# Waiting for the last four stores in a second section of SyncE alone

## The chip, the cores and the metric

One core of a Trainium2 chip. The metric is device time in microseconds (us) of one execution. "Span" is the time from the first to the last of the program's own instructions in a profiled execution; the device time is longer than it, by 1.79 us on average in the 11 runs of the kernel before that were timed beside e1. The same kernel scatters by more than the change is expected to be worth (the same 11 runs lie between 210.50 and 211.92 us), so the argument rests on the instruction records of the profiles, and the timed runs are a check.

## The reference

```python
# x [16, 512, 1024], weight [1024, 768], bias [768], residual [16, 512, 768], all float32
def reference(x, weight, bias, residual):
    return (np.matmul(x, weight) + bias + residual).astype(np.float32)
```

## The kernel before

The rows of x (8192 of 1024) go through the core in 64 tiles of 128. Each is cast to bf16, transposed on TensorE, multiplied by the weights, and finished by VectorE (with additions on GpSimd). SyncE issues all transfers. The kernel first collects its operations in a list and then emits them in one section of all engines, with waits that it works out itself; every transfer gets a semaphore (a counter that engines can wait for) of its own, which its landing raises by 16 (that of the last store rises 16 times in the trace, from 206.243 to 207.725). A section ends with a row of small instructions, called its exit here. In the trace of this kernel SyncE raises a signal at 208.036 us, every engine answers it with a DRAIN and a semaphore at about 208.1 (drains start at 208.074 to 208.126), SyncE collects the answers with two waits (208.211 and 208.270) and passes a NOP (208.336, 13 ns).

The store part and the end (cuts marked with "..."):

```python
# the order of the stores: kind, block, first and last row group (and a cut in partitions)
 ... ('s', 0, 0, 16), ... ('s', 1, 0, 16), ... ('s', 2, 0, 16), ('s', 3, 0, 10), ('s', 3, 10, 11, 104),
 ('s', 3, 11, 13), ('s', 3, 13, 14), ('s', 3, 14, 15), ('c', 3, 15, 0), ('c', 3, 15, 1)]

    def emit(self):                         # of the class Program
        ...                                 # which waits are already known to be over
        for n, (eng, emit, _, dma) in enumerate(ops):
            e = self.engines[eng]
            for d in waits[n]:
                e.wait_ge(*mark[d])
            if emit is None:                # the collecting operation: waits only
                continue
            ins = emit(e)
            if dma:
                sem = self.tc.alloc_semaphore(f"landed_{n}")
                mark[n] = (sem, 16)
                ins.then_inc(sem, 16)
            ...

                    dma(out_d[S, p0:p1, j0:j1, n0:n0 + nl],            # a store
                        R[p0:p1, t0 % RR:t0 % RR + j1 - j0, n0:n0 + nl],
                        rows(t0, t0 + j1 - j0, cs), [("out", len(stores))])
                    stores.append(("out", len(stores)))
    ...
    op("sp", None, stores)                  # SyncE waits for all stores
    with tc.tile_critical():                # one section of all engines
        prog.emit()
# the tile context closes here: drain, barrier, clearing of semaphores, barrier
```

There are eleven stores (the one with a cut counts twice). The last four are a row group of 384 KB, another, and the two pieces of the last row group, 256 KB and 128 KB.

Of the kernel before, what the change touches and what calls it, by code (L numbers as in the profile page):

```python
# [14 lines left out]
RR = 32  # L15
# [18 lines left out]
 ('r', 2, 6, 16), ('s', 1, 0, 16), ('x', 3, 0, 6), ('r', 3, 0, 7), ('x', 3, 6, 16),  # L34
 ('r', 3, 7, 16), ('s', 2, 0, 16), ('s', 3, 0, 10), ('s', 3, 10, 11, 104), ('s', 3, 11, 13),
 ('s', 3, 13, 14), ('s', 3, 14, 15), ('c', 3, 15, 0), ('c', 3, 15, 1)]
LAST = [(0, 512), (512, 256)]


class Program:  # L40
# [10 lines left out]
    def add(self, eng, emit, rd=(), wr=(), dma=False):  # L51
        n, ops = len(self.ops), self.ops
        deps = {self.writer[k] for k in (*rd, *wr) if k in self.writer and (eng != "pe" or ops[self.writer[k]][0] != eng)}
        for k in wr:
            deps.update(d for d in self.readers.get(k, ()) if ops[d][0] != eng or ops[d][3])
        for k in rd:
            self.readers.setdefault(k, set()).add(n)
        for k in wr:
            self.writer[k], self.readers[k] = n, set()
        self.ops.append((eng, emit, deps - {n}, dma))  # L60

    def emit(self):
        ops, known = self.ops, {e: {} for e in self.engines}
        lane, count, snap, waits = [], {}, [], []
        for n, (eng, _, deps, dma) in enumerate(ops):
            mine = (n, 0) if dma else (eng, count.setdefault(eng, 0) + 1)
            if not dma:
                count[eng] += 1
            seen = known[eng]
            need = {}  # L70
            for d in deps:
                f, i = lane[d]
                if seen.get(f, -1) < i and i > need.get(f, (-1, 0))[0]:
                    need[f] = (i, d)
            need = {
                f: (i, d) for f, (i, d) in need.items()
                if not any(snap[d2].get(f, -1) >= i for g, (_, d2) in need.items() if g != f)
            }
            for f, (i, d) in need.items():
                for g, v in (*snap[d].items(), (f, i)):  # L80
                    if seen.get(g, -1) < v:
                        seen[g] = v
            waits.append([d for _, d in need.values()])
            lane.append(mine)
            own = dict(seen)
            own[mine[0]] = mine[1]
            snap.append(own)
        told = {d for w in waits for d in w}
        sems = {e: self.tc.alloc_semaphore(f"done_{e}") for e in self.engines if e != "sp"}
        total, mark = dict.fromkeys(self.engines, 0), {}  # L90
        for n, (eng, emit, _, dma) in enumerate(ops):
            e = self.engines[eng]
            for d in waits[n]:
                e.wait_ge(*mark[d])
            if emit is None:
                continue
            ins = emit(e)
            if dma:
                sem = self.tc.alloc_semaphore(f"landed_{n}")
                mark[n] = (sem, 16)  # L100
                ins.then_inc(sem, 16)
            elif n in told:
                total[eng] += 1
                mark[n] = (sems[eng], total[eng])
                ins.then_inc(sems[eng], 1)


@with_exitstack
def kernel(
# [8 lines left out]
    nc = tc.nc  # L118
# [33 lines left out]
    prog = Program(tc)  # L152
    op = prog.add

    def rows(a, b, cs=range(len(chunks))):
        return [("R", r % RR, c) for r in range(a, b) for c in cs]

    def dma(dst, src, rd, wr):
        op("sp", lambda e: e.dma_start(out=dst, in_=src), rd, wr, dma=True)  # L159
# [3 lines left out]
    stores = []  # L163

    def pump():
        while queue:
            kind, S, j0, j1, *cut = queue[0]
            if kind == "c":
                need = [("outc", j1)]
            elif kind in ("w", "b"):  # L170
                need = []
            elif kind == "x":
                need = [("cast", t - XR) for t in range(J * S + j0, J * S + j1) if t >= XR]
            elif kind == "r":
                need = [("store", t - RR) for t in range(J * S + j0, J * S + j1) if t >= RR]
                at = [t % RR for t in range(J * S + j0, J * S + j1)]
                if S < RR // J and any(W_ROW <= r < W_ROW + 2 * n_q for r in at):
                    need.append(("wcast", n_q - 1))
                if S < RR // J:
                    need += [("add", t) for t in range(EARLY_END) if TMP_ROW + t in at]  # L180
            else:
                need = [("out", J * S + j) for j in range(j0, j1)]
            if not all(n in done for n in need):
                return
            queue.pop(0)
            t0, nj = J * S + j0, j1 - j0
            if kind == "b":
                dma(bias_row.rearrange("(g p) n -> g p n", p=QUAD)[:, 0, :],
                    bias[None, :].to_broadcast([P // QUAD, N]), [], ["bias_row"])
                continue  # L190
            if kind == "w":
                dma(w_st[:, 2 * S + j0:2 * S + j1, :], w_d[:, S, j0:j1, :], [],
                    rows(W_ROW + 2 * S + j0, W_ROW + 2 * S + j1))
                continue
            if kind == "x":
                dma(X[:, t0 % XR:t0 % XR + nj, :], x_d[S, :, j0:j1, :], [],
                    [("X", t % XR) for t in range(t0, t0 + nj)])
            elif kind == "r":
                dma(R[:, t0 % RR:t0 % RR + nj, :], res_d[S, :, j0:j1, :], [], rows(t0, t0 + nj))
            else:  # L200
                n0, nl = (0, N) if kind == "s" else LAST[j1]
                cs = range(len(chunks)) if kind == "s" else [j1]
                j1 = j1 if kind == "s" else j0 + 1
                edges = [0, *cut, P]
                for p0, p1 in zip(edges, edges[1:]):
                    dma(out_d[S, p0:p1, j0:j1, n0:n0 + nl],
                        R[p0:p1, t0 % RR:t0 % RR + j1 - j0, n0:n0 + nl], rows(t0, t0 + j1 - j0, cs), [("out", len(stores))])
                    stores.append(("out", len(stores)))
                done.update(("store", J * S + j) for j in range(j0, j1))
            done.update((kind, J * S + j) for j in range(j0, j1))  # L210

    def mark(*what):
        done.add(what)
        pump()
# [31 lines left out]
    def times(po, lhsT, rhs, first, final, rd, wr):  # L246
        def emit(e):
            return e.add_instruction(mybir.InstMatmult(  # L248
                name=nc.get_next_instruction_name(),
                ins=[e.lower_ap(rhs), e.lower_ap(lhsT, for_matmul_weights=True)], outs=[e.lower_ap(po)],  # L250
                start_tensor_calc=first, stop_tensor_calc=final,
                tile_size=(P, P), tile_position=(0, 0), ldweights=False,
            ))
        op("pe", emit, rd, wr)
# [46 lines left out]
    def dummies(n, i):  # L301
# [10 lines left out]
        out=ident, in_=ident, compare_op=mybir.AluOpType.not_equal, fill=1.0, base=0,  # L312
        pattern=[[-1, P]], channel_multiplier=1,
    ), ["ident"], ["ident"])
    dummies(WARM, 0)

    pump()
    for kind, *a in HEAD_ORDER:
        if kind == "bias":
# [15 lines left out]
        else:  # L335
            mm_all(a[0], [a[1]])
    pump()
    for t in range(HEAD - 1):
        if ("fin", t) not in done:
# [11 lines left out]
    t = n_t - 1  # L351
    for i, (n0, nl) in enumerate(LAST):
        b = (t - 2 * i) % HEAD
# [5 lines left out]
    mark("out", t)  # L359
    pump()  # L360
    assert not queue, queue
    op("sp", None, stores)
    with tc.tile_critical():  # L363
        prog.emit()


# [28 lines left out]
```

## Time and profile before

| | before |
|---|---|
| device time, first measurement, median of 4 runs | 210.88 us (210.72 to 211.20) |
| span of the profiled run | 209.394 us |
| last matmul ends | 204.088 us |
| the last store's landing (16th increment of its semaphore) | 207.725 us |
| from that landing to the end of the span | 1.669 us |

The prediction shows the lines of the profile that carry this, and how to read them. The times with three decimals are from the single instruction and semaphore records of the same trace.

### The profile page before, as it was taken

What the parts mean: (1) busy time and instruction counts of PE and PEld (TensorE: products, weight loads), DVE (VectorE), ACT (ScalarE), POOL (GpSimd) and SP (SyncE); (2) the same over time, 40 slices, a digit from 0 to 9 for tenths busy, and PEclk for the clock granted to TensorE, in tenths of its full rate; (3) what the DMA queues carried; (4) which work ended last, traced back from release to release, by engine and by line L of the source; (5) the groups of instructions that cost most, each with busy time, mean ns of one, the idle gap of its engine ahead of it and who ended that gap; (6) DMA issues with size and microseconds to landing.
All of it is one profiled execution on the core that took longest, in us unless ns stands there. A gap on an engine that the chain in (4) does not pass through costs nothing.

```text
span 209.4 us, 2487 instructions
## 1 busy us (share of the span) xinstructions
PE 202.3 (97%) x1298; PEld 81.2 (39%) x794; DVE 105.3 (50%) x141; ACT 66.2 (32%) x69; POOL 115.2 (55%) x71
## 2 busy tenths in 40 slices
PE   7999999999999999999999999999999999999990
PEld 2433433443444344344434433443444344334440
DVE  1458555445545554554455454645544554554460
ACT  2444513412740372310370083320190055330000
POOL 1100029759999805998039702999108940999000
PEclk9999999999999999999999999999999999999999
DMA  6999999999989899999999999999999999998993
GB/s 214 426 425 440 434 417 467 389 446 419 491 376 501 379 438 393 441 446 416 419 446 480 394 411 495 404 394 421 434 469 415 446 404 475 432 451 382 417 364 145
DMA packets 4924, 87.20 MB, mean 416 GB/s; under 512 B 557, under 2 KB 685, under 8 KB 1841
## 3 DMA queue, kind: packets, MB, share of 16 engines
q1 hardware_dynamic: 4913, 87.05, 97.6%
q8 instruction: 8, 0.13, 0.3%
q14 instruction: 3, 0.02, 0.0%
HBM read 61.88 MB, written 25.17 MB: 416 GB/s over the span
## 4 chain that ended last, share of the span: by engine, by line
PE 92%; DMA 4%; DVE 1%; SPq 0%; ACT 0%; issue 0%
PE psum_o L248 79%; PE pt L241 13%; DMA x_tile<-in_x_dram 4%; SPq L159 0%; DVE xt L217 0%; ACT xb L217 0%; DVE ro L220 0%; SPq L390 0%; SPq L363 0%
## 5 line engine op out<-in xcount | busy, mean ns | idle before, releaser
L248 PE MATMUL psum_o<-w_sb,xt 128*128 128x256 bf16 (+1 forms) x1024 | 176.6, 326 | 0.3 <-DVE xt L217 0.3
L220 POOL TENSOR_TENSOR ro<-ro,bias_sb 128x768 f32<-128x768 f32 x50 | 88.9, 1813 | 46.7 <-DMA ro<-in_residual_dram 46.7
L217 ACT CAST xb<-x_tile 128x1024 bf16<-128x1024 f32 (+1 forms) x63 | 61.4, 1023 | 117.1 <-DMA x_tile<-in_x_dram 81.8
L259 PEld LDWEIGHTS <-xt 128*128 128x128 bf16 x520 | 50.9, 98 | 102.5 <-issue 100.5
L217 DVE COPY xt<-pt 128x1024 bf16<-128x1024 bf16 x64 | 44.1, 691 | 84.0 <-PE pt L241 84.0
L220 DVE TENSOR_TENSOR ro<-psum_o,ro 128x768 f32<-128x768 f32 (+2 forms) x51 | 47.6, 934 | 6.3 <-POOL ro L220 4.3
L241 PE MATMUL pt<-ident,xb 128*128 128x128 f32 x256 | 38.7, 275 | 0.2 <-ACT xb L217 0.2
L220 POOL TENSOR_TENSOR ro<-ro 128x768 f32<-128x768 f32 x14 | 25.0, 1818 | 25.0 <-DMA ro<-in_residual_dram 25.0
L241 PEld LDWEIGHTS pt<-ident,xb 128*128 128x128 f32 x256 | 30.1, 142 | 15.4 <-issue 12.3
L220 DVE TENSOR_TENSOR ro<-psum_o,bias_sb 128x768 f32<-128x768 f32 x14 | 13.2, 948 | 0.0
L303 PE MATMUL psum_o<-warm 128*128 128x512 bf16 x18 | 6.9, 546 | 1.4 <-DVE warm_a L223 1.4
L217 DVE CAST xb<-x_tile 128x512 bf16<-128x512 f32 (+1 forms) x4 | 1.9, 492 | 5.8 <-DMA x_tile<-in_x_dram 5.8
L217 ACT CAST w_sb<-ro 128x768 bf16<-128x768 f32 x4 | 3.3, 832 | 3.7 <-DMA ro<-in_weight_dram 3.7
L217 POOL CAST w_sb<-ro 128x768 bf16<-128x768 f32 x1 | 0.8, 824 | 6.0 <-DMA ro<-in_weight_dram 6.0
L303 PEld LDWEIGHTS psum_o<-warm 128*128 128x128 bf16 x18 | 2.2, 127 | 4.7 <-issue 3.0
L217 DVE CAST w_sb<-ro 128x768 bf16<-128x768 f32 x3 | 1.7, 558 | 2.0 <-DMA ro<-in_weight_dram 2.0
L217 ACT ACT_TABLE_LOAD x1 | 1.3, 1283 | 0.9 <-SPq L363 0.9
L320 DVE STREAM_SHUFFLE bias_sb<-bias_row 128x768 f32<-128x768 f32 x1 | 1.0, 1008 | 0.0
L223 DVE MEMSET warm<- 128x256 uint32 x1 | 0.3, 272 | 1.1 <-SPq L363 1.1
L223 DVE MEMSET bias_row<- 128x768 f32 x1 | 0.7, 698 | 0.1
L223 POOL MEMSET ident<- 128x128 f32 x1 | 0.2, 205 | 0.5 <-SPq L363 0.5
L311 POOL TENSOR_SCALAR_AFFINE_SELECT ident<-ident 128x128 f32<-128x128 f32 x1 | 0.3, 294 | 0.2 <-POOL ident L223 0.2
(7 smaller groups left out, 0.7 us busy)
## 6 DMA issues: line engine op xcount, KB each, us to landing
out_dram<-ro SPq DMA_DIRECT2D x3, 6144.0 KB, 34.4
x_tile<-in_x_dram SPq DMA_DIRECT2D x3, 5120.0 KB, 24.5
ro<-in_residual_dram SPq DMA_DIRECT2D x3, 3840.0 KB, 32.0
x_tile<-in_x_dram SPq DMA_DIRECT2D x3, 3072.0 KB, 39.8
ro<-in_residual_dram SPq DMA_DIRECT2D x3, 2304.0 KB, 18.5
x_tile<-in_x_dram SPq DMA_DIRECT2D x4, 1024.0 KB, 10.9
x_tile<-in_x_dram SPq DMA_DIRECT2D x2, 2048.0 KB, 23.3
out_dram<-ro SPq DMA_DIRECT2D x1, 3840.0 KB, 13.1
```

The lines of the kernel that those rows point to most:

```text
L217: op(eng, lambda e: (e.copy if eng == "act" else e.tensor_copy)(out=dst, in_=src), rd, wr)
L220: op(eng, lambda e: e.tensor_add(out=dst, in0=a, in1=b), rd, wr)
L223: op(eng, lambda e: e.memset(dst, v), [], [wr])
L241: op("pe", lambda e, q=q: e.transpose(out=pt[:, q, :], in_=words[:, ts(q, P)], identity=ident), [("XB", t % XB_N, 2 * q // n_q), "ident"], ...
L248: return e.add_instruction(mybir.InstMatmult(name=nc.get_next_instruction_name(), ins=[e.lower_ap(rhs), e.lower_ap(lhsT, for_matmul_weight ...
L259: op("pe", lambda g: g.ldweights(lhsT), rd)
L303: op("pe", lambda e: e.matmul(PO[i][:, 0:512], lhsT=warm[:, 0:P], rhs=warm, start=True, stop=True), ["warm"], [("PO", i)])
L311: op("pool", lambda e: e.affine_select(out=ident, in_=ident, compare_op=mybir.AluOpType.not_equal, fill=1.0, base=0, pattern=[[-1, P]], ch ...
L320: op("dve", lambda e: e.stream_shuffle(out=bias_sb, in_=bias_row, mask=[0] * QUAD), ["bias_row"], ["bias"])
```

## The change

Its intent: SyncE waits at the end of the big section only for the first seven stores. The section then closes, with all its drains and answers, while the last four stores are still in flight, and these are awaited in a second section that names SyncE alone, the last store first.

```diff
+OUTSIDE = 4
-    def emit(self):
+    def emit(self, ends):
...
-            if emit is None:
-                continue
             ins = emit(e)
...
+        return [mark[n] for n in ends]
...
-                        R[...], rows(...), [("out", len(stores))])
-                    stores.append(("out", len(stores)))
+                        R[...], rows(...), [])
+                    stores.append(len(prog.ops) - 1)
...
-    op("sp", None, stores)
     with tc.tile_critical():
-        prog.emit()
+        landed = prog.emit(stores)
+        for sem, value in landed[:-OUTSIDE]:
+            nc.sync.wait_ge(sem, value)
+    with tc.tile_critical(sync_engine=mybir.EngineType.SP):
+        for sem, value in reversed(landed[-OUTSIDE:]):
+            nc.sync.wait_ge(sem, value)
```

More of the change, by code (lines that the diff above doesn't have):

```diff
@@ L206, in pump @@
                     dma(out_d[S, p0:p1, j0:j1, n0:n0 + nl],
-                        R[p0:p1, t0 % RR:t0 % RR + j1 - j0, n0:n0 + nl], rows(t0, t0 + j1 - j0, cs), [("out", len(stores))])
-                    stores.append(("out", len(stores)))
+                        R[p0:p1, t0 % RR:t0 % RR + j1 - j0, n0:n0 + nl], rows(t0, t0 + j1 - j0, cs), [])
+                    stores.append(len(prog.ops) - 1)
                 done.update(("store", J * S + j) for j in range(j0, j1))
```

## The prediction

> **What bounds the kernel now.** I read the page from the top, then the stretch after the last matmul in growing detail, because the change touches only what SyncE does there.
>
> First the page's head and its chain of work.
>
> ```profile
> span 209.4 us, 2487 instructions
> PE 202.3 (97%) x1298; PEld 81.2 (39%) x794; DVE 105.3 (50%) x141; ACT 66.2 (32%) x69; POOL 115.2 (55%) x71
> ...
> PE 92%; DMA 4%; DVE 1%; SPq 0%; ACT 0%; issue 0%
> ```
>
> TensorE is busy for 202.3 of 209.4 us and carries 92% of the chain; its clock row reads 9 in every slice. None of these instructions is touched. What can move is the part in which TensorE is idle, and only the end of it: 209.4 - 202.3 = 7.1 us are idle in all, some of them at the start (first matmul at 1.4 us) and 5.3 at the end. The table of busy time by stretch shows the end:
>
> ```profile
> 203.00:204.10 1.10, 1.09 (x9) 0.69 (x7) 0.69 (x1) 0.00 (x0) 0.00 (x0) 1.00 1.00 405
> 204.10:205.00 0.90, 0.00 (x0) 0.00 (x0) 0.42 (x1) 0.00 (x0) 0.00 (x0) 1.00 0.83 330
> 205.00:206.00 1.00, 0.00 (x0) 0.00 (x0) 0.00 (x0) 0.00 (x0) 0.00 (x0) 1.00 0.98 373
> 206.00:207.00 1.00, 0.00 (x0) 0.00 (x0) 0.00 (x0) 0.00 (x0) 0.00 (x0) 1.00 0.29 102
> 207.00:208.00 1.00, 0.00 (x0) 0.00 (x0) 0.00 (x0) 0.00 (x0) 0.00 (x0) 1.00 0.02 8
> 208.00:209.40 1.40, 0.00 (x0) 0.00 (x0) 0.00 (x0) 0.00 (x0) 0.00 (x0) 0.73 0.00 0
> ```
>
> The columns are the stretch, its length, busy time of PE, PEld, DVE, ACT and POOL, granted clock, DMA share and GB/s. Matmuls end at 204.1, the last addition of VectorE at 204.55 (0.42 us from 204.125), and after that only bytes and semaphores move: nearly no data after 207, none after 208, and still the program ends at 209.4. So the last 5.3 us fall into three parts: last addition and store (to about 207.7), and then roughly 1.7 us without data or compute. That last part is the subject.
>
> The instructions of the waiting line, of the section's line and of the line that closes the program, from 204 us on, say what it consists of:
>
> ```profile
> L94 SPq EVENT_SEMAPHORE  x4: 28/28/28, 205.8 to 207.8; - x4
> L363 SPq COMPARE_BRANCH  x1: 33/33/33, 207.9 to 207.9; - x1
> L363 ACTq DRAIN  x1: 8/8/8, 208.1 to 208.1; - x1
> L363 POOLq DRAIN  x1: 41/41/41, 208.1 to 208.1; - x1
> L363 SPq EVENT_SEMAPHORE  x3: 17/28/28, 208.0 to 208.3; - x3
> L363 SPq NOP  x1: 13/13/13, 208.3 to 208.3; - x1
> ...
> L390 SPq DRAIN  x3: 7/7/7, 208.4 to 208.7; - x3
> L390 POOLq EVENT_SEMAPHORE_RANGE_CLEAR  x1: 287/287/287, 208.8 to 208.8; - x1
> L390 POOLq EVENT_SEMAPHORE  x4: 17/17/17, 208.5 to 209.3; - x4
> ```
>
> Each row has durations (least, median, most) in ns and the first and last start in us. L94 are SyncE's waits for the stores; L363 is the section's exit, in which SyncE tells every engine to drain and collects the answers; L390 closes the whole program: a barrier, the clearing of the semaphores by GpSimd, a second barrier. The rows of waits of SyncE's queue say that the stores set the start of it:
>
> ```profile
> SPq L94 <- DMA out_dram<-ro: 2.7, 3, 0.9
> SPq L390 <- PEq L390: 0.8, 2, 0.6
> ```
>
> The single instruction records give the order to the nanosecond. The last store (128 KB) is issued at 204.578 and its 16th and last increment comes at 207.725, 3.15 us later, and 0.76 us after the 15th. Then: wait at 207.741, one more wait at 207.806, branch at 207.873, signal to all engines 208.036, SyncE's own drain 208.126, two collecting waits at 208.211 and 208.270, closing NOP 208.336, first drain of the program's end 208.411, its barrier 208.474, end 209.394. From the landing to the end: 0.311 us of waits and branch (207.725 to 208.036), 0.375 us of section exit (208.036 to 208.411), 0.983 us of program end. Sum 1.669 us.
>
> [...]the drains and waits report 7 to 28 ns on SyncE, but successive ones start 59 to 90 ns apart, so I count starts, not durations. [...]the last store's semaphore rises 16 times between 206.243 and 207.725, and SyncE goes on at 207.741. [...]
>
> **The change part by part.**
> 1. The stores no longer write a key of their own, and the collecting operation at the end is gone. No other operation read those keys, so no wait elsewhere changes. Worth 0.
> 2. At the end of the first section SyncE now waits for the first seven of eleven stores. Before, nine waits stood there (the first two of the eleven had been awaited by later loads): four instructions with two waits each, and one on the branch. Of the seven, the last to land is the store of two rows: its semaphore's last increment came at 204.860, and SyncE itself is busy until 204.967 with issuing the last store. So these waits find everything done. Three or four instructions of about 0.065 us, a branch of 0.163 us and the exit of 0.375 us: 204.97 + 0.26 + 0.16 + 0.38 = about 205.8. All of this runs while the last four stores are in flight.
> 3. Entry to the second section: a NOP and a branch, as at the program's beginning (NOP at 0.720, branch at 0.796, first DMA issue at 0.949: 0.23 us). 205.8 + 0.23 = 206.0. The last landing is at 207.725, so 1.7 us of slack: it hides, even if the entry cost three times that.
> 4. Four waits, in reverse order, so that the last store's semaphore is asked first, with the next to last. Two instructions or one and the branch: landing 207.725, wait 207.741, second 207.806, branch 207.873, next 208.036. That is the very sequence of before, where the last landing also was followed by exactly one more wait and the branch. Gain 0 (0.065 at most, if the packing leaves one instruction less).
> 5. The exit of a section of SyncE alone. This is where I expect the gain. The two collecting waits (208.211 and 208.270) have nobody to collect: 208.336 - 208.211 = 0.125 us. If the signal to the engines and SyncE's drain on its own signal go too, 208.211 - 208.036 = 0.175 us more. So 0.125 to 0.300, middle 0.21.
> 6. The program's end: 0.983 us, unchanged. The other engines' drains for its first barrier came at 208.157 to 208.193 and would now come near 205.9, but that barrier opens only with SyncE's at 208.474, so earlier arrivals are worth nothing. The clearing gets a few semaphores more: 46 of them took 0.239 us from first to last, 5.3 ns each; one to five more cost 0.01 to 0.03 us.
>
> Sum: -0.21 + 0.02 = -0.19 us, from 210.84 to 210.65 us, 0.09%.
>
> **The rivals.** The first is that the second section's exit goes to all engines after all. For it: the exit of the first section serves all engines, and the drains of the program's end are there in any case. Against it: the section names SyncE alone, and nothing of another engine stands in it. Time: then step 5 is worth 0, and with step 6's clearing it is 210.86.
>
> The second is that the whole exit and some of the program's end hide behind the stores, as the intent of the change suggests: 0.375 us of exit, or even the first barrier too. For the exit: SyncE may need only a NOP after its waits. Against the barrier: the page's chain and the waits show SyncE as the last to arrive in it, and SyncE must still wait for the stores before. Time: 210.84 - 0.37 = 210.47, and no view speaks for more.
>
> The third is a cost that I can't see beforehand: the second block begins elsewhere in SyncE's stream[...]. SyncE runs only 57 instructions within the span and its branches took 0.15 and 0.16 us here, so no stall shows. The entry branch would be hidden by the 1.7 us anyway, and only the exit branch counts[...].
>
> The fourth is chance: the 16th increment 0.76 us behind the 15th shows how much the last landing can shift from one execution to another, more than the change is worth. The three runs before lie 0.48 us apart.
>
> **Range and chances.** Steps 1 to 4 and 6 are near 0, step 5 lies between 0 and -0.37, and the scatter of a median adds about 0.2 either way, from the runs' 0.48. That gives 210.25 to 211.0. A change by 2% would be 4.2 us, two and a half times the whole 1.67 us between the last landing and the end; it can't be saved there, and it would have to be lost in something that nothing here shows. So 0.98 for within 2%, and 0.01 for either side.
>
> **What would show it right or wrong.** Right: drains of ACT, POOL, DVE and PE for the section at about 205.5 to 205.9 instead of 208.1; SyncE's waits for the last stores still ending at the last landing; from that landing to the end about 1.46 to 1.56 us instead of 1.67; TensorE's 202.3 us and all rows of transfers as before. Wrong: another set of drains of all engines after the landing (first rival), a distance under 1.4 us (second), a gap over 0.2 us after SyncE's last branch (third), or a last landing counted from the last store's issue that differs from 3.15 us by more than 0.2 us (fourth: then the difference of the times is not the change's).

That the time between span and device time stays as it is was my assumption; it was 1.79 us in the profiled run of before (211.18 and 209.394) and 1.78 us in that of the changed kernel (210.92 and 209.142).

## The result, and the profile after

Median 210.87 us (210.35 to 210.92, 4 runs) against 210.88 us of before (210.72 to 211.20, 4 runs). Ratio 0.9992, 95% interval 0.9973 to 1.0012. A ratio is the mean time of one kernel's fast runs over that of the other's of the same rounds, so it is not quite the ratio of the medians. By the clock alone this is no change. The profile shows one.

The head of the changed kernel's page:

```profile
span 209.1 us, 2471 instructions
...
PE 200.4 (96%) x1273; PEld 80.9 (39%) x794; DVE 105.3 (50%) x141; ACT 66.1 (32%) x69; POOL 115.1 (55%) x71
```

The weight loads and the instructions of the other engines are equal in number. TensorE's 25 fewer matmuls are records missing from the trace, not work that went: both kernels compile to the same 1298 multiplications and 794 weight loads. The 1.9 us less of busy time follow from that and mean nothing; the last matmul ends at 204.093 (before 204.088).

The busy time by stretch, with the columns as in the prediction (the last two are DMA share and GB/s):

```profile
206.00:207.00 1.00, 0.00 (x0) 0.00 (x0) 0.00 (x0) 0.00 (x0) 0.00 (x0) 0.95 0.33 117
207.00:208.00 1.00, 0.00 (x0) 0.00 (x0) 0.00 (x0) 0.00 (x0) 0.00 (x0) 0.50 0.02 8
208.00:209.20 1.20, 0.00 (x0) 0.00 (x0) 0.00 (x0) 0.00 (x0) 0.00 (x0) 0.50 0.00 0
```

The data end as before: 8 GB/s in the microsecond from 207 on, nothing after 208. The gain lies in what follows them. Rows of the first section's line from 204 us on (least, median and most ns, first and last start in us):

```profile
L363 SPq COMPARE_BRANCH  x1: 33/33/33, 205.4 to 205.4; - x1
L363 ACTq DRAIN  x1: 8/8/8, 205.6 to 205.6; - x1
...
L363 SPq NOP  x1: 13/13/13, 205.9 to 205.9; - x1
```

All of it stood between 207.9 and 208.3 before. It now runs beside the stores. The second section's line has no row of any engine but SyncE:

```profile
L367 SPq NOP  x2: 13/13/13, 206.0 to 208.1; - x2
L367 SPq EVENT_SEMAPHORE  x1: 17/17/17, 208.0 to 208.0; - x1
L367 SPq DRAIN  x1: 7/7/7, 208.0 to 208.0; - x1
```

And these are rows of the line that closes the program; the waits for the last four stores are booked on it too:

```profile
L395 SPq EVENT_SEMAPHORE  x7: 17/28/622, 206.0 to 209.1; - x7
...
L395 ACTq DRAIN  x2: 8/8/8, 205.7 to 208.5; - x2
...
L395 SPq COMPARE_BRANCH  x1: 33/33/33, 207.8 to 207.8; - x1
L395 POOLq EVENT_SEMAPHORE_RANGE_CLEAR  x1: 287/287/287, 208.6 to 208.6; - x1
```

ScalarE's first drain for the closing barrier comes at 205.7 (before 208.2), as the other engines' do, and gains nothing: the second is at 208.5, when SyncE is there. The clearing takes the 287 ns that it took before. One row is unexpected, a wait instruction of 622 ns. The single records explain it. In the records, SyncE's wait instructions for the stores carry two semaphores each. The four stores' waits stand in the second section's entry, each paired with a semaphore of the section itself that had been complete for long (the last of these rose at 205.991), and in the order of landing, not reversed:

| SyncE, changed kernel | start (us) | took (ns) | the store that it waits for lands at (us) |
|---|---|---|---|
| wait, with the fourth last store | 206.098 | 28 | 205.807 |
| wait, with the third last | 206.160 | 622 | 206.759 |
| wait, with the next to last | 206.813 | 608 | 207.399 |
| wait, with the last | 207.456 | 308 | 207.741 |
| branch | 207.801 | 33 | |
| signal of the exit | 207.956 | 17 | |
| drain, NOP, first drain of the program's end | 208.041, 208.115, 208.159 | 7, 13, 7 | |

In all four, the store is the second semaphore of the pair. The three that really wait report 622, 608 and 308 ns and end 0.022 to 0.023 us after the landing.

From the last landing to the end, step by step:

| us | before | after | difference |
|---|---|---|---|
| landing to the exit's signal (waits, branch) | 0.311 | 0.215 | -0.096 |
| signal to the program's end's first drain (exit) | 0.375 | 0.203 | -0.172 |
| the program's end | 0.983 | 0.983 | 0 |
| sum | 1.669 | 1.401 | -0.268 |

The last store was issued at 204.584 and landed 3.157 us later (before: 204.578 and 3.147), so here the two traces can be compared without a correction, and the spans differ by 0.252 us.

### The profile page after: what moved, and what is told of

Read it like the earlier page. It is cut to its first block, busy times and chain, and to the rows that moved or that the text cites. A ratio compares the mean times of both kernels' runs of the same rounds, so it can differ in the third digit from the quotient of the medians.

```text
span 209.1 us, 2471 instructions
## 1 busy us (share of the span) xinstructions
PE 200.4 (96%) x1273; PEld 80.9 (39%) x794; DVE 105.3 (50%) x141; ACT 66.1 (32%) x69; POOL 115.1 (55%) x71
## 4 chain that ended last, share of the span: by engine, by line
PE 91%; DMA 4%; issue 1%; DVE 1%; SPq 0%; ACT 0%
PE psum_o L249 78%; PE pt L242 13%; DMA x_tile<-in_x_dram 4%; SPq L160 0%; DVE xt L218 0%; ACT xb L218 0%; DVE ro L221 0%; SPq L395 0%; SPq L363 0%
## 5 line engine op out<-in xcount | busy, mean ns | idle before, releaser
L304 PE MATMUL psum_o<-warm 128*128 128x512 bf16 x18 | 6.4, 514 | 1.4 <-DVE warm_a L224 1.4
L321 DVE STREAM_SHUFFLE bias_sb<-bias_row 128x768 f32<-128x768 f32 x1 | 1.0, 1024 | 0.0
```

The source lines that it names most:

```text
L304: op("pe", lambda e: e.matmul(PO[i][:, 0:512], lhsT=warm[:, 0:P], rhs=warm, start=True, stop=True), ["warm"], [("PO", i)])
L321: op("dve", lambda e: e.stream_shuffle(out=bias_sb, in_=bias_row, mask=[0] * QUAD), ["bias_row"], ["bias"])
```

## The experiments

Theory A is that the 0.27 us are instructions of SyncE that no longer stand behind the last landing, and nothing else. Its rivals: B, that it is chance in the landing; and, step by step, that the gain is only the second section's, or only the early exit's, or comes from the early arrival of the other engines. All kernels gave correct results. A second section without the name of SyncE wasn't run, because its compiled program is equal to the changed kernel's on every engine: what counts is that only SyncE has work in the section, not that the source names it.

### e1: the changed kernel again, five rounds

> The changed kernel again, unaltered, for its size against the scatter. Theory A (the distance from the last landing to the end of the span shrank from 1.669 to 1.401 us by fewer instructions of SyncE behind the landing, and nothing else moved): the same 1.40 us distance within 0.02 in this profile, and the timed runs 0.27 us (0.13%) below before, to be seen only if the mean of 5 rounds is good to 0.1 us. Rival B (the difference of the two spans is chance in the last landing): a distance that differs by over 0.1 us from 1.40, or timed runs at a ratio of 1.000 or above.

Landing to end 1.401 us, the same to the nanosecond, in a trace whose stores landed quite differently. Timed: mean of 6 runs 210.89 us against 211.14 us (11 runs of before), ratio 0.9987, interval 0.9967 to 1.0007. The size is the expected one, but the interval still contains 1. Yet the span of the profiled run was 208.6 us, 0.5 us shorter than in the first profile: the last store landed 2.53 us after its issue instead of 3.16. So rival B is wrong on the difference inside the program, and right in that chance of this kind is larger than the change.

### e2: one section, the waits in the order of issue

```diff
-        for sem, value in landed[:-OUTSIDE]:
+        for sem, value in landed:
             nc.sync.wait_ge(sem, value)
-    with tc.tile_critical(sync_engine=mybir.EngineType.SP):
-        for sem, value in reversed(landed[-OUTSIDE:]):
-            nc.sync.wait_ge(sem, value)
```

> No second section: all eleven stores awaited at the end of the first, in the order of issue, so that the last store stands in the last wait instruction. Tells the order of the waits from the second section. Theory A: the wait behind the last landing goes (0.065 us), the exit to all engines stays 0.375 us, so landing to end 1.60 us, and the engines' drains come at about 208.0 us. Rival (the whole gain is the second section's): 1.67 us.

Landing to end 1.609 us. The row of the waits from 204 us on:

```profile
L366 SPq EVENT_SEMAPHORE  x5: 28/28/28, 205.2 to 207.8; - x5
```

Here the last store is the first semaphore of its pair, and all five waits report 28 ns. The last of the five starts at 207.822, 0.017 us after the landing at 207.805, and the branch follows at 207.887. So 0.060 of the 0.268 us come from the order alone: in the kernel before, the wait for the last store was the third of four. The other 0.208 us need the second section. Timed: ratio 0.9995, interval 0.9970 to 1.0019, which shows nothing at this size.

### e3: all engines in the second section

```diff
         for sem, value in reversed(landed[-OUTSIDE:]):
             nc.sync.wait_ge(sem, value)
+        for e in (nc.tensor, nc.vector, nc.scalar, nc.gpsimd):
+            e.wait_ge(*landed[0])
```

> The changed kernel with one wait in its second section for each of TensorE, VectorE, ScalarE and GpSimd, for the first store's semaphore that was complete long before. So the second section's exit collects from all engines again. Theory A: exit 0.375 instead of 0.203 us, landing to end 1.57 us. Rival (the gain is in the waits or in the early arrival at the first section's exit, not in who is in the second section): 1.40 us.

Landing to end 1.535 us, between the two, and nearer to theory A. The rows of the second section's line:

```profile
L367 SPq EVENT_SEMAPHORE  x3: 17/28/28, 208.2 to 208.4; - x3
L367 SPq NOP  x2: 13/13/13, 206.1 to 208.4; - x2
L367 ACTq DRAIN  x1: 8/8/8, 208.2 to 208.2; - x1
L367 POOLq DRAIN  x1: 34/34/34, 208.2 to 208.2; - x1
```

The drains of the other engines are back behind the landing (207.935), and so are two collecting waits of SyncE. Exit 0.337 instead of 0.203 us: 0.134 us are what it costs to collect from all. The 0.038 us that I had too much: the second section's closing NOP and the drain after it stand closer together (0.048 us) than in the one-section kernel (0.075), and the instruction after SyncE's drain follows 0.012 us sooner. By the records, the NOP of the one-section kernel raises a semaphore that the drain waits for, and here it doesn't; that this is the reason wasn't tested. Landing to signal is 0.215 us, as in the changed kernel. Timed: ratio 0.9991, interval 0.9968 to 1.0014, again nothing to see.

So the 0.268 us are 0.060 for the order of the waits, 0.036 for the form of the last wait (below), 0.134 for collecting from nobody, and 0.038 for the shorter close of the second section, which is read from the records alone.

### e5, e6, e7: one store, two, or all eleven in the second section

```diff
-OUTSIDE = 4
+OUTSIDE = 1      # and 2, and 11
```

> Only the last store is left to the second section; the first awaits the other ten. The store before the last lands 0.34 us before the last, and from that landing SyncE still has the wait, the branch, the first section's exit (0.31 us to its closing NOP), the second's entry and five waits to run: in the changed kernel's steps 0.08 + 0.16 + 0.31 + 0.55 = 1.10 us to the second exit's signal. Theory A (the first exit is free only as long as the stores in flight outlast it): the signal comes 1.10 - 0.34 = 0.76 us after the last landing instead of 0.215, so landing to end about 1.94 us, longer than the 1.67 of before. Rival (a second section of SyncE alone pays by itself): 1.40 us.

> The last two stores in the second section. The third last lands 0.98 us before the last, the same 1.10 us of steps follow: theory A expects the signal at 0.22 us (0.12 by the chain from the third last, so the last landing sets it again), landing to end 1.40 to 1.45 us. Rival as for the run with one store: 1.40 too, so only together with that run does it tell something.

> All eleven stores in the second section, none awaited at the end of the first. Theory A: nothing more is hidden than with four, landing to end 1.40 us, unless the longer list of waits (17 instead of 10) is put behind the last store's wait: 0.065 us for each instruction that stands there, at most 0.25 us.

With one store outside, landing to end was 1.897 us, longer than before the change. The second section's line in that run:

```profile
L367 SPq NOP  x2: 13/13/13, 207.6 to 208.1; - x2
L367 SPq EVENT_SEMAPHORE  x1: 17/17/17, 208.0 to 208.0; - x1
```

The entry's NOP comes at 207.6, and the last store had landed at 207.263. So SyncE was still busy with the first section's exit, and the wait for the last store, started at 207.754, found it done. The signal came 1.044 us after the landing of the next to last store (expected 1.10). Timed: ratio 1.0017, interval 0.9999 to 1.0035, mean 211.18 against 210.84 us; the trace's 0.23 us lie in it. A second section is no gain in itself.

With two outside, 1.403 us; with all eleven, 1.420 us (one look each). The wait for the last store in the run with two started at 207.864, 0.117 us ahead of the landing at 207.981, so two is just enough, in this landing. From two to eleven nothing moves by more than 0.02 us, and the four of the change leave room: in its trace the first wait that really waits starts at 206.160.

### e4: the last four stores awaited behind the program's end

If instructions behind the last landing are all that there is, the exit and the program's end can go in front of it as well. The four semaphores are allocated before the tile context, so that its clearing leaves them alone, and SyncE waits for them as its last instructions.

```diff
-                sem = self.tc.alloc_semaphore(f"landed_{n}")
+                sem = late[ends[-OUTSIDE:].index(n)] if n in ends[-OUTSIDE:] else self.tc.alloc_semaphore(f"landed_{n}")
...
-    with tc.tile_critical(sync_engine=mybir.EngineType.SP):
-        for sem, value in reversed(landed[-OUTSIDE:]):
-            nc.sync.wait_ge(sem, value)
...
+    late = [nc.alloc_semaphore(f"late_{i}") for i in range(OUTSIDE)]
     with _tile.TileContext(nc) as tc:
-        tile_matmul_bias_add_kernel(tc, *args)
+        tile_matmul_bias_add_kernel(tc, *args, late)
+    for sem in reversed(late):
+        nc.sync.wait_ge(sem, 16)
```

> No second section: the last four stores' semaphores are allocated outside of the program's own clearing and awaited by SyncE behind the program's closing barriers, as its last instructions. If, as theory A says, everything behind the last landing is instructions that SyncE could have had out of the way, then exit (0.375 us) and end (0.983 us) run from about 205.6 to 207.0 us beside the stores in flight and landing to end falls from 1.40 to about 0.05 us: span 207.8 us, timed 1.3 us below the changed kernel, 1.6 us (0.75%) below before. Rival (what comes after the span takes the gain back): span 207.8 but timed as the changed kernel within 0.3 us.

Landing to end 0.023 us, span 207.3 us. First the line that closes the program, then the waits:

```profile
L394 POOLq EVENT_SEMAPHORE  x4: 17/17/17, 205.8 to 206.6; - x4
...
L394 POOLq EVENT_SEMAPHORE_RANGE_CLEAR  x1: 268/268/268, 206.1 to 206.1; - x1
```

```profile
L397 SPq EVENT_SEMAPHORE  x2: 280/291/302, 206.7 to 207.0; - x2
```

The second barrier is over at 206.6, and the last store landed at 207.284. Timed: mean 208.88 us (6 runs) against 211.14 us, ratio 0.9894, interval 0.9873 to 0.9915: 1.1% faster than before, and 2.0 us below the changed kernel's 210.89 us, measured in the same rounds. This kernel beats both, and by more than I expected. Behind the span there remain 1.34 us on average instead of 1.79 us, so the rival is wrong: what follows the span doesn't take the gain back but adds 0.45 us to it.

It leans on one thing that the two others don't: its four semaphores are not cleared by the program. Behind the program, the traces show a row of updates over nearly all semaphores (in the kernel before from 210.053 to 210.720, its span's end being at 209.394). I take it to be their clearing, from its place and order alone. In e4's trace this row reaches three of the four at 207.878 to 207.891, after the span's end at 207.307. For the fourth there is no record (some are missing in a trace: that of before shows 14 and 13 of the sixteen increments of two stores); in the trace of e8, whose semaphores are allocated alike, it is updated at 209.178, after the end of that span too.

### e8: every engine waits behind the end

```diff
     for sem in reversed(late):
         nc.sync.wait_ge(sem, 16)
+    for e in (nc.tensor, nc.vector, nc.scalar, nc.gpsimd):
+        e.wait_ge(late[-1], 16)
```

> The kernel of e4 with a wait for the last store on TensorE, VectorE, ScalarE and GpSimd too, behind the closing barriers. e4 was timed 2.24 us below before, 0.6 more than the span's own tail gave, and the time between span and measured time fell from 1.79 to 1.34 us (means of its runs). Theory A2 (in e4 the other engines have gone on to what follows the program while SyncE waits): here that difference is 1.79 us again, the landing to end at most 0.1 us, and the timed runs 0.45 us above e4. Rival (the difference shrinks because of the order of the program's instructions, or by chance): 1.34 us again, timed as e4.

Landing to end 0.079 us, and the difference between time and span is 1.80 us again (4 runs, 1.77 to 1.84). The waits of the others, at the landing (208.015):

```profile
L399 ACTq EVENT_SEMAPHORE  x1: 17/17/17, 208.0 to 208.0; - x1
L399 POOLq EVENT_SEMAPHORE  x1: 17/17/17, 208.0 to 208.0; - x1
```

So the 0.45 us of e4 are the other engines' head start into what follows the program. The records agree: after the program, a semaphore that none of its instructions names is raised nine times in a first group (in the kernel before from 209.629 to 210.157). In e4 the first four come between 206.910 and 207.193, while SyncE is still waiting, and the fifth 0.116 us after the span's end; in e8 the first comes at 208.289, after everyone's wait, and in the kernel before the fifth comes 0.542 us after the span's end. Timed: mean 209.61 us against 210.84 us of before, ratio 0.9938 (0.9915 to 0.9960). I expected 0.45 us above e4; by the ratios it is 0.44% or 0.93 us. The rest isn't in the difference of time and span. These were two chips, and the landings scatter as the next table shows; I haven't separated the two.

### What scatters

The span is the first multiplication with weights (its start), plus the matmuls, plus the way from the last matmul to the last landing, plus the way from there to the end:

| profile | first multiplication | last matmul's end | to the last landing | landing to end | span | last increment behind the 15th |
|---|---|---|---|---|---|---|
| before | 8.487 | 204.088 | 3.637 | 1.669 | 209.394 | 0.762 |
| after | 8.462 | 204.093 | 3.648 | 1.401 | 209.142 | 0.511 |
| e1, after again | 8.595 | 204.221 | 3.022 | 1.401 | 208.644 | 0.106 |
| e2 | 8.522 | 204.283 | 3.522 | 1.609 | 209.414 | 0.672 |
| e3 | 8.648 | 204.270 | 3.665 | 1.535 | 209.470 | 0.711 |
| e4 | 8.445 | 204.091 | 3.193 | 0.023 | 207.307 | 0.011 |
| e5 | 8.590 | 204.201 | 3.062 | 1.897 | 209.160 | 0.169 |
| e6 | 8.641 | 204.262 | 3.719 | 1.403 | 209.384 | 0.519 |
| e7 | 8.621 | 204.257 | 3.263 | 1.420 | 208.940 | 0.271 |
| e8 | 8.564 | 204.208 | 3.807 | 0.079 | 208.094 | 0.538 |

The head moves the end by 0.2 us and the last landing by 0.8 us, three times the change. Where the last landing is late, one share of the store is late: fifteen of sixteen increments are there up to 0.76 us earlier. In the trace of before, the 1024-byte packets that end last run from 207.040 to 207.382 one after another, with a 4-byte packet behind them ending at 207.387, 0.338 us before the last increment; the other shares had their last packet of the store before 206.7. The share was late before this store: in the trace of before, the last increment comes 0.012 us behind the one before it in the store that landed at 201.437, 0.631 us in the next one (the first piece of the store with a cut), and 0.731 to 0.768 us in each of the last five; in e1 these five have 0.091 to 0.160. So in this trace the lag comes about ahead of the last matmul, and of everything that the change touches. What makes one share late in some executions, I haven't tried.

## Why the prediction was right or wrong

The range (210.25 to 211.0) and the judgement "within 2%" hold, and the sum behind them, -0.19 us, was of the right size: -0.268 us by the trace, and -0.08% to -0.13% by the two timings, each of which would also fit no change at all. The range would have held without any gain too, since it contains the 210.84 us of before. That the sum came so close is partly luck: step 4 gave 0.096 us that I had put at 0, step 5 gave 0.038 less than its middle of 0.21, and the 0.02 us of step 6 didn't come. One sign of being right was missed: landing to end was to be 1.46 to 1.56 us, and it is 1.401. Without step 4's 0.096 it would have been 1.497, inside. It is also just above the 1.4 us under which I wanted to believe the second rival, but here the records decide: the second section's exit stands behind the landing (signal at 207.956). The predicted median, 210.65, was missed by 0.22 us, which is scatter and not a finding.

**Steps 1 to 3** (nothing elsewhere moves; the first section's exit and the second's entry hide) hold. The exit's NOP came at 205.9, 0.1 us later than worked out, since the last store's issue took 588 instead of 389 ns in that run. The run with one store outside shows that the slack was the condition.

**Step 4** (the waits, gain 0, at most 0.065) failed: they gave 0.096 us. I counted "exactly one more wait and the branch" after the last landing, because I took the reversed order of the source for the order of the instructions. In the trace the four waits stand in the entry, in the order of landing, with the last store in the last pair (207.456). That gave 0.060 us, shown with one section in order. The remaining 0.036 us come with the form of the pair: the changed kernel's last wait has already started when the store lands, and the branch follows 0.060 us after the landing; with the store as the pair's first semaphore, it follows after 0.082 us, and the signal another 0.008 us later than in the changed kernel. These two add to 0.030; the other 0.006 us are the few nanoseconds by which equal steps differ from run to run (the two collecting waits of the same exit start 0.059 us apart before and 0.065 after). That the form is the cause was only argued from equal traces; no run changed it alone.

**Step 5** (the exit, 0.125 to 0.300) held with 0.172 us. The part for which I gave a reason, two waits with nobody to collect from, was 0.125 by my sum and 0.134 by the run with all engines. The other 0.038 us are neither of the two terms that I had named. The signal and SyncE's own drain did not go, which the upper bound would have needed.

**Step 6** (the end unchanged, 0.01 to 0.03 us more to clear) held for the 0.983 us. The clearing got nothing longer, 287 ns in both: the second section uses the first one's semaphores again.

**The rivals.** The exit to all engines: wrong for this kernel, and brought about on purpose it costs 0.134 us. The whole exit and part of the end hidden behind the stores: not by this change, but the idea was worth most of all. I had set it aside because SyncE "must still wait for the stores before" the closing barrier; it must only wait before the program ends. A stall at the second block: none, the branch took 0.155 us. Chance in the landing: it is larger than the change, as I said, and the profile of e1 shows it.

The 3.15 us between the last store's issue and its landing: The trace of before shows the late share's first packet at 207.040, 2.46 us after the issue and behind a row of the 2048-byte packets of the store before (206.474 to 207.034), and 0.34 us from the end of its last packet (207.387) to the semaphore (207.725); in the changed kernel this last way is 0.33 us (207.410 to 207.741). So 2.46 of the 3.15 us in this trace lie before the late share's first packet.

## What to carry to other kernels

Write down every instruction between the last landing and the end of the program, and ask of each whether it needs the data to have landed; here only one wait does (e4: landing to end 0.023 us). Here, moving closing work in front of the last wait paid only as long as the transfers in flight outlasted it (two stores were enough, 1.403 us from landing to end; one made it worse, 1.897 against 1.669 of before), and the waits' order must be read from the compiled program or the trace, not from the source (reversed there, in the order of landing in the trace of the changed kernel). Where the change is smaller than the scatter of the runs (here 0.27 against 1.42 us), measure it between two events of one trace.
